# Attention over 384 short heads: loads as fp32 on the sync queue in chunks of 32 heads, casts on GpSimd, groups of 8 heads with wide evacuations and a three-stage pipeline

## The chip, the cores and the metric

The kernel runs on one core of a Trainium2 chip. The metric is device time in microseconds, the median of several runs.

The engines are PE (TensorE, matmuls and transposes; PEld is its weight load), DVE (VectorE), ACT (ScalarE), POOL (GpSimd) and SP (SyncE, which only issues DMAs here). Data move between HBM and SBUF through 16 DMA engines. "Sync queue", "scalar queue" and "GpSimd queue" say which engine issued a DMA; a DMA that changes the data type is issued from GpSimd in these kernels.

## The reference

```python
batch, n_heads, seq, head_dim = 32, 12, 128, 64     # fp32 inputs, drawn times 0.1
scores = scale * np.matmul(q, k.transpose(0, 1, 3, 2))
attn = np.exp(scores - scores_max)
attn = attn / (np.sum(attn, axis=-1, keepdims=True) + 1e-8)
return np.matmul(attn, v).astype(np.float32)
```

There are 384 heads of 128 x 64. A row of a head is 64 fp32, so 256 bytes; with the sequence on the 128 partitions, each partition reads one 256-byte run per head. Three inputs and one output make 50.33 MB.

## The kernel before

One batch entry (12 heads) at a time: casting DMAs bring q, k and v to SBUF as bf16. Pairs of heads are transposed by PE, the transposes copied out of PSUM one by one (q by ACT, k by DVE), scores formed transposed for four heads, one exp over them, outputs for two heads at a time with a 65th column of ones in v that yields the sum of the row, and one division at the end.

```python
    q_bf = pbf.tile([128, H, D], bf16, tag="q_bf")
    nc.gpsimd.dma_start(out=q_bf, in_=qr[b])             # casts while it moves; k and v alike
    for p in range(NP):
        nc.tensor.transpose(qt_ps, q_bf[:, p * HT:(p + 1) * HT, :]..., ident)
        nc.scalar.copy(qt[:, p, :], qt_ps)               # 128 x 128
        nc.tensor.transpose(kt_ps, k_bf[...], ident)
        nc.vector.tensor_copy(kt[:, p, :], kt_ps)
    for g in range(H // HX):                             # HX = 4
        ...                                              # four matmuls into sT_ps
        nc.scalar.activation(out=attnT, in_=sT_ps[:, :, :128], func=Exp, scale=scale)
        for gg in range(HX // HO):                       # HO = 2
            ...                                          # two matmuls into o_ps
            nc.vector.tensor_copy(o_b[...], o_ps[:, :, :D + 1])
    nc.vector.reciprocal(recip, o_b[:, :, D:D + 1])
    nc.vector.tensor_mul(o_sb, o_b[:, :, :D], recip.to_broadcast([128, H, D]))
    nc.sync.dma_start(out=orr[b], in_=o_sb)
```

Every PSUM pool has one buffer. The order of instructions on each engine is chosen by the framework's scheduler.

The softmax here doesn't subtract the row's maximum and nothing guards it: scores larger than these inputs give would overflow.

## Time and profile before

| | before |
|---|---|
| device time (226.3 in the later rounds with the changed kernel) | 226.2 us |
| PE / DVE / ACT / POOL busy | 168.3 / 120.2 / 99.7 / 101.5 us |
| read from and written to HBM | 37.75 + 12.58 MB, 224 GB/s over the span |
| chain of work that ended last | PE 64%, ACT 17%, DVE 9%, DMA 2% |

Busy time adds up instructions that may wait inside the pipeline, so the chain, not the busy share, says what bounds. The lines themselves are shown in the prediction below. One more view, the page's list of DMA queues (packets, MB written, and the time that the packets took as a share of 16 engines' span):

```profile
q0 software_dynamic: 148992, 18.88, 131.9%
q1 hardware_dynamic: 49664, 12.58, 31.0%
```

q0 carries the casting loads: 147,456 data packets of 128 bytes written (256 read). q1 carries the stores, 49,152 packets of 256 bytes. The share goes above 100%, so the times of packets in one engine overlap.

### The profile page before, as it was taken

The page shows a single profiled execution, that of the slowest core. Times are in us where ns is not written, and L with a number is a line of the kernel's source. Part 1 is how long each engine was busy: PE and PEld are TensorE (multiplying, and loading weights), DVE is VectorE, ACT ScalarE, POOL GpSimd, SP SyncE. Part 2 cuts the span into 40 slices and gives each one's busy share as a digit, 9 for nine tenths or more (in the row PEclk, how much of TensorE's full clock was granted, in tenths as well). Part 3 has the DMA queues.
Part 4 walks back from the last instruction along what each step waited for, and adds up shares of the span by engine and source line. Part 5 has one row for each costly group of instructions (what it writes and reads, how often), then busy time and mean ns, then how long its engine had stood idle before and what let it go on. Part 6 is the DMA issues. An engine that isn't in the chain of part 4 may idle for free.

```text
span 224.4 us, 3513 instructions
## 1 busy us (share of the span) xinstructions
PE 168.3 (75%) x1152; PEld 83.1 (37%) x1152; DVE 120.2 (54%) x448; ACT 99.7 (44%) x289; POOL 101.5 (45%) x134
## 2 busy tenths in 40 slices
PE   0688787788787787877787877788877778878750
PEld 0344333344333343333343333444333334333330
DVE  0264555664555564555564555565555565456652
ACT  2554545445544445444445444444444444444320
POOL 8963455534475443455443455543355534222000
DMA  7999999999999999999999999999999999999333
GB/s 50 149 156 184 148 142 140 155 148 166 151 153 161 161 159 166 148 149 141 129 151 167 146 148 134 137 154 167 149 146 144 135 150 161 142 110 134 76 69 71
DMA packets 198674, 31.69 MB, mean 141 GB/s; under 512 B 198656, under 2 KB 198656, under 8 KB 198656
## 3 DMA queue, kind: packets, MB, share of 16 engines
q0 software_dynamic: 148992, 18.88, 131.9%
q1 hardware_dynamic: 49664, 12.58, 31.0%
q8 instruction: 9, 0.15, 0.3%
q14 instruction: 9, 0.07, 0.1%
HBM read 37.75 MB, written 12.58 MB: 224 GB/s over the span
## 4 chain that ended last, share of the span: by engine, by line
PE 64%; ACT 17%; DVE 9%; issue 6%; DMA 2%; ACTq 0%; POOL 0%; POOLq 0%
PE sT_ps L84 26%; PE qt_ps L63 14%; PE o_ps L103 14%; PE kt_ps L70 11%; ACT attnT L92 9%; ACT qt L68 7%; DVE o_b L110 5%; DVE kt L75 3%; DMA q_bf<-in_q_dram 2%; DVE o_sb L118 1%; ACTq L92 0%; DVE recip L116 0%; POOL ident masks.py:197 0%; POOLq masks.py:199 0%; POOLq L134 0%
## 5 line engine op out<-in xcount | busy, mean ns | idle before, releaser
L68 ACT COPY qt<-qt_ps 128x128 bf16<-128x128 bf16 x192 | 50.4, 263 | 69.0 <-PE qt_ps L63 69.0
L75 DVE COPY kt<-kt_ps 128x128 bf16<-128x128 bf16 x192 | 42.8, 223 | 70.8 <-PE kt_ps L70 66.1
L84 PE MATMUL sT_ps<-qt,kt 64*128 64x128 bf16 x384 | 71.5, 282 | 12.2 <-ACT attnT L92 11.5
L92 ACT ACTIVATE attnT<-sT_ps 128x512 bf16<-128x512 f32 x96 | 57.3, 597 | 47.7 <-PE sT_ps L84 42.9
L63 PE MATMUL qt_ps<-ident,q_bf 128*128 128x128 bf16 x192 | 54.2, 282 | 26.8 <-ACT qt L68 21.4
L110 DVE COPY o_b<-o_ps 128x130 f32<-128x130 f32 x192 | 55.6, 289 | 29.2 <-PE o_ps L103 28.9
L103 PE MATMUL o_ps<-v_bf,attnT 128*128 128x65 bf16 x384 | 56.8, 242 | 6.1 <-DVE o_b L110 6.1
L70 PE MATMUL kt_ps<-ident,k_bf 128*128 128x128 bf16 x192 | 56.4, 294 | 5.3 <-DVE kt L75 4.5
L84 PEld LDWEIGHTS <-kt 64*128 64x128 bf16 x384 | 26.4, 101 | 61.1 <-issue 43.0
L103 PEld LDWEIGHTS <-attnT 128*128 128x128 bf16 x384 | 34.3, 120 | 34.4 <-issue 26.5
L56 POOL MEMSET v_bf<- 128x12 bf16 x32 | 5.0, 155 | 79.9 <-PE o_ps L103 79.9
L52 POOL DMA_DIRECT2D q_bf<-in_q_dram x32 | 32.6, 1020 | 10.2 <-PE qt_ps L63 8.9
L57 POOL DMA_DIRECT2D v_bf<-in_v_dram x32 | 32.6, 1018 | 9.9 <-POOL v_bf L56 9.9
L54 POOL DMA_DIRECT2D k_bf<-in_k_dram x32 | 32.8, 1025 | 1.4 <-PE kt_ps L70 1.4
L63 PEld LDWEIGHTS <-q_bf 128*128 128x128 bf16 x192 | 18.9, 113 | 31.4 <-issue 15.7
L118 DVE TENSOR_TENSOR o_sb<-o_b,recip 128x768 f32<-128x768 f32 x32 | 30.3, 948 | 0.0
L70 PEld LDWEIGHTS <-k_bf 128*128 128x128 bf16 x192 | 23.2, 121 | 8.7 <-issue 0.9
L116 DVE RECIPROCAL recip<-o_b 128x12 f32<-128x12 f32 x32 | 7.0, 219 | 0.0
L68 ACT ACT_TABLE_LOAD x1 | 1.3, 1283 | 0.7 <-PEq L134 0.7
masks.py:199 POOL TENSOR_SCALAR_AFFINE_SELECT ident<-ident 128x128 bf16<-128x128 bf16 x1 | 0.3, 305 | 0.1
masks.py:197 POOL MEMSET ident<- 128x128 bf16 x1 | 0.2, 204 | 0.3 <-POOLq L134 0.3
L134 POOL MEMSET const-float32-0.0<- 128x1 f32 x1 | 0.1, 98 | 0.2 <-issue 0.2
(3 smaller groups left out, 0.3 us busy)
## 6 DMA issues: line engine op xcount, KB each, us to landing
out_dram<-o_sb SPq DMA_DIRECT2D x32, 384.0 KB, 5.7
q_bf<-in_q_dram POOLq DMA_DIRECT2D x32, 192.0 KB, 5.9
k_bf<-in_k_dram POOLq DMA_DIRECT2D x32, 192.0 KB, 6.4
v_bf<-in_v_dram POOLq DMA_DIRECT2D x32, 192.0 KB, 5.1
```

What stands on the lines that cost most here:

```text
L52: nc.gpsimd.dma_start(out=q_bf, in_=qr[b])
L54: nc.gpsimd.dma_start(out=k_bf, in_=kr[b])
L57: nc.gpsimd.dma_start(out=v_bf[:, :, :D], in_=vr[b])
L63: nc.tensor.transpose(qt_ps, q_bf[:, p * HT:(p + 1) * HT, :].rearrange("a b c -> a (b c)"), ident,)
L68: nc.scalar.copy(qt[:, p, :], qt_ps)
L70: nc.tensor.transpose(kt_ps, k_bf[:, p * HT:(p + 1) * HT, :].rearrange("a b c -> a (b c)"), ident,)
L75: nc.vector.tensor_copy(kt[:, p, :], kt_ps)
L84: nc.tensor.matmul(sT_ps[:, i, :128], lhsT=kt[j * D:(j + 1) * D, p, :], rhs=qt[j * D:(j + 1) * D, p, :], start=True, stop=True,)
L92: nc.scalar.activation(out=attnT, in_=sT_ps[:, :, :128], func=mybir.ActivationFunctionType.Exp, bias=0.0, scale=scale,)
L103: nc.tensor.matmul(o_ps[:, i, :D + 1], lhsT=attnT[:, gg * HO + i, :], rhs=v_bf[:, h, :], start=True, stop=True,)
L110: nc.vector.tensor_copy(o_b[:, g * HX + gg * HO:g * HX + (gg + 1) * HO, :], o_ps[:, :, :D + 1],)
L118: nc.vector.tensor_mul(o_sb, o_b[:, :, :D], recip.to_broadcast([128, H, D]))
```

## The change

Its intent is to replace many small instructions by few wide ones and to keep loads off GpSimd's queue. Loads become fp32 DMAs of 32 heads on the sync queue, with a cast by GpSimd after each. Groups of 8 heads are evacuated at once: one copy of 1024 bf16 for the transposes, one exp over 1024, one reciprocal and one multiplication straight from PSUM. Transposes of group s, scores of group s-1 and outputs of group s-2 follow each other in a fixed order. Stores also go by the sync queue, and the loads of chunk c+3 stand behind the store of chunk c.

```diff
-        nc.gpsimd.dma_start(out=q_bf, in_=qr[b])
+            nc.sync.dma_start(out=x, in_=src[:, sl, :])          # x: fp32, 32 heads
...
+        nc.gpsimd.tensor_copy(q_bf, q_f)                         # k and v alike
...
-            nc.scalar.copy(qt[:, p, :], qt_ps)
-            nc.vector.tensor_copy(kt[:, p, :], kt_ps)
+            nc.vector.tensor_copy(qkt, t_ps)                     # 8 heads of q and k
...
-                nc.vector.tensor_copy(o_b[...], o_ps[:, :, :D + 1])
+            nc.vector.reciprocal(recip, ov[:, :, :, D])
+            nc.vector.tensor_mul(o_sb[...], ov[:, :, :, :D], recip.to_broadcast([128, 2, HP, D]))
+            if r == GPC - 1:
+                nc.sync.dma_start(out=orr[:, c * CH:(c + 1) * CH, :], in_=o_sb)
+                if c + 3 < NCH:
+                    load(c + 3)
+        for s in range(NG + 2):
+            if s < NG:
+                stage_a(s)                                       # transposes, one copy
+            if 0 <= s - 1 < NG:
+                stage_b(s - 1)                                   # scores, exp
+            if 0 <= s - 2 < NG:
+                stage_c(s - 2)                                   # outputs, division
```

(The transposes and scores have two PSUM buffers, the outputs one.)

More of the change, by code (lines that the diff above doesn't have):

```diff
@@ L26, with heads @@
     scale = 1.0 / (D ** 0.5)
-    HT = 128 // D
-    NP = H // HT
-    HX = 4
-    HO = 2
-    BANK = 512
-    qr = q.rearrange("b h s d -> b s h d")
-    kr = k.rearrange("b h s d -> b s h d")
-    vr = v.rearrange("b h s d -> b s h d")
-    orr = out.rearrange("b h s d -> b s h d")
-    singles = ctx.enter_context(tc.tile_pool(name="singles", bufs=1))
+    N = B * H
+    CH = 32
+    NCH = N // CH
+    GH = 8
+    NG = N // GH
+    GPC = CH // GH
+    HP = GH // 2
+    def heads(x):
+        return x.rearrange("b h s d -> s (b h) d")
@@ new lines @@
+    qr, kr, vr, orr = heads(q), heads(k), heads(v), heads(out)
+    singles = ctx.enter_context(tc.tile_pool(name="singles", bufs=1))
+    pin = ctx.enter_context(tc.tile_pool(name="pin", bufs=3))
+    pbf = ctx.enter_context(tc.tile_pool(name="pbf", bufs=3))
+    pt = ctx.enter_context(tc.tile_pool(name="pt", bufs=3))
+    pa = ctx.enter_context(tc.tile_pool(name="pa", bufs=3))
+    po = ctx.enter_context(tc.tile_pool(name="po", bufs=3))
+    ps_t = ctx.enter_context(tc.tile_pool(name="ps_t", bufs=2, space=bass.MemoryType.PSUM))
@@ L39 @@
+    ps_s = ctx.enter_context(tc.tile_pool(name="ps_s", bufs=2, space=bass.MemoryType.PSUM))
+    ps_o = ctx.enter_context(tc.tile_pool(name="ps_o", bufs=1, space=bass.MemoryType.PSUM))
     ident = singles.tile([128, 128], bf16)
     make_identity(nc, ident)
-    pbf = ctx.enter_context(tc.tile_pool(name="pbf", bufs=3))
-    pt = ctx.enter_context(tc.tile_pool(name="pt", bufs=3))
-    pa = ctx.enter_context(tc.tile_pool(name="pa", bufs=6))
-    po = ctx.enter_context(tc.tile_pool(name="po", bufs=2))
@@ L46 @@
-    ps_t = ctx.enter_context(tc.tile_pool(name="ps_t", bufs=1, space=bass.MemoryType.PSUM))
-    ps_s = ctx.enter_context(tc.tile_pool(name="ps_s", bufs=1, space=bass.MemoryType.PSUM))
-    ps_o = ctx.enter_context(tc.tile_pool(name="ps_o", bufs=1, space=bass.MemoryType.PSUM))
-    for b in range(B):
-        q_bf = pbf.tile([128, H, D], bf16, tag="q_bf")
-        nc.gpsimd.dma_start(out=q_bf, in_=qr[b])
-        k_bf = pbf.tile([128, H, D], bf16, tag="k_bf")
-        nc.gpsimd.dma_start(out=k_bf, in_=kr[b])
-        v_bf = pbf.tile([128, H, D + 1], bf16, tag="v_bf")
-        nc.gpsimd.memset(v_bf[:, :, D:D + 1], 1.0)
-        nc.gpsimd.dma_start(out=v_bf[:, :, :D], in_=vr[b])
-        qt = pt.tile([128, NP, 128], bf16, tag="qt")
-        kt = pt.tile([128, NP, 128], bf16, tag="kt")
-        for p in range(NP):
-            qt_ps = ps_t.tile([128, 128], bf16, tag="qt_ps")
-            nc.tensor.transpose(
-                qt_ps,
-                q_bf[:, p * HT:(p + 1) * HT, :].rearrange("a b c -> a (b c)"),
-                ident,
-            )
-            nc.scalar.copy(qt[:, p, :], qt_ps)
-            kt_ps = ps_t.tile([128, 128], bf16, tag="kt_ps")
-            nc.tensor.transpose(
-                kt_ps,
-                k_bf[:, p * HT:(p + 1) * HT, :].rearrange("a b c -> a (b c)"),
-                ident,
-            )
-            nc.vector.tensor_copy(kt[:, p, :], kt_ps)
-        o_b = po.tile([128, H, D + 1], f32, tag="o_b")
-        for g in range(H // HX):
-            sT_ps = ps_s.tile([128, HX, BANK], f32, tag="sT")
-            for i in range(HX):
-                h = g * HX + i
-                p, j = divmod(h, HT)
-                nc.tensor.matmul(
-                    sT_ps[:, i, :128],
-                    lhsT=kt[j * D:(j + 1) * D, p, :],
-                    rhs=qt[j * D:(j + 1) * D, p, :],
-                    start=True,
-                    stop=True,
-                )
-            attnT = pa.tile([128, HX, 128], bf16, tag="attnT")
-            nc.scalar.activation(
-                out=attnT,
-                in_=sT_ps[:, :, :128],
-                func=mybir.ActivationFunctionType.Exp,
-                bias=0.0,
-                scale=scale,
-            )
-            for gg in range(HX // HO):
-                o_ps = ps_o.tile([128, HO, BANK], f32, tag="o_ps")
-                for i in range(HO):
-                    h = g * HX + gg * HO + i
-                    nc.tensor.matmul(
-                        o_ps[:, i, :D + 1],
-                        lhsT=attnT[:, gg * HO + i, :],
-                        rhs=v_bf[:, h, :],
-                        start=True,
-                        stop=True,
-                    )
-                nc.vector.tensor_copy(
-                    o_b[:, g * HX + gg * HO:g * HX + (gg + 1) * HO, :],
-                    o_ps[:, :, :D + 1],
-                )
-        recip = po.tile([128, H], f32, tag="recip")
-        nc.vector.reciprocal(recip, o_b[:, :, D:D + 1])
-        o_sb = po.tile([128, H, D], f32, tag="o_sb")
-        nc.vector.tensor_mul(o_sb, o_b[:, :, :D], recip.to_broadcast([128, H, D]))
-        nc.sync.dma_start(out=orr[b], in_=o_sb)
@@ new lines, with load, cast @@
+    chunks = {}
+    raw = {}
+    def load(c):
+        sl = slice(c * CH, (c + 1) * CH)
+        tiles = []
+        for src, tag in ((qr, "q_f"), (kr, "k_f"), (vr, "v_f")):
+            x = pin.tile([128, CH, D], f32, tag=tag, name=tag)
+            nc.sync.dma_start(out=x, in_=src[:, sl, :])
+            tiles.append(x)
+        raw[c] = tiles
+    def cast(c):
+        q_f, k_f, v_f = raw.pop(c)
+        q_bf = pbf.tile([128, CH, D], bf16, tag="q_bf", name="q_bf")
+        nc.gpsimd.tensor_copy(q_bf, q_f)
+        k_bf = pbf.tile([128, CH, D], bf16, tag="k_bf", name="k_bf")
+        nc.gpsimd.tensor_copy(k_bf, k_f)
+        v_bf = pbf.tile([128, CH, D + 1], bf16, tag="v_bf", name="v_bf")
+        nc.gpsimd.memset(v_bf[:, :, D:D + 1], 1.0)
+        nc.gpsimd.tensor_copy(v_bf[:, :, :D], v_f)
+        chunks[c] = (q_bf, k_bf, v_bf)
@@ new lines, with stage_a, stage_b, stage_c @@
+    with tc.manual_schedule():
+        qkts, attns, osbs = {}, {}, {}
+        for c in range(3):
+            load(c)
+        cast(0)
+        def stage_a(i):
+            c, r = divmod(i, GPC)
+            q_bf, k_bf, v_bf = chunks[c]
+            t_ps = ps_t.tile([128, 2, HP, 128], bf16, tag="t_ps", name="t_ps")
+            for p in range(HP):
+                for j, x in enumerate((q_bf, k_bf)):
+                    h = GH * r + 2 * p
+                    nc.tensor.transpose(
+                        t_ps[:, j, p, :], x[:, h:h + 2, :].rearrange("p h d -> p (h d)"), ident)
+            qkt = pt.tile([128, 2, HP, 128], bf16, tag="qkt", name="qkt")
+            nc.vector.tensor_copy(qkt, t_ps)
+            qkts[i] = qkt
+        def stage_b(i):
+            qkt = qkts.pop(i)
+            s_ps = ps_s.tile([128, 2, HP, 128], f32, tag="s_ps", name="s_ps")
+            for p in range(HP):
+                for j in range(2):
+                    pr = slice(j * D, (j + 1) * D)
+                    nc.tensor.matmul(s_ps[:, j, p, :], lhsT=qkt[pr, 1, p, :],
+                                     rhs=qkt[pr, 0, p, :], start=True, stop=True)
+            attn = pa.tile([128, 2, HP, 128], bf16, tag="attn", name="attn")
+            nc.scalar.activation(out=attn, in_=s_ps, func=mybir.ActivationFunctionType.Exp,
+                                 bias=0.0, scale=scale)
+            attns[i] = attn
+        def stage_c(i):
+            c, r = divmod(i, GPC)
+            attn = attns.pop(i)
+            v_bf = chunks[c][2]
+            o_ps = ps_o.tile([128, 2, 512], f32, tag="o_ps", name="o_ps")
+            ov = o_ps[:, :, :HP * (D + 1)].rearrange("p j (h e) -> p j h e", h=HP)
+            for h in range(GH):
+                nc.tensor.matmul(ov[:, h // HP, h % HP, :], lhsT=attn[:, h % 2, h // 2, :],
+                                 rhs=v_bf[:, GH * r + h, :], start=True, stop=True)
+            if r == 0:
+                osbs[c] = po.tile([128, CH, D], f32, tag="o_sb", name="o_sb")
+            o_sb = osbs[c]
+            recip = pa.tile([128, 2, HP], f32, tag="recip", name="recip")
+            nc.vector.reciprocal(recip, ov[:, :, :, D])
+            nc.vector.tensor_mul(
+                o_sb[:, GH * r:GH * (r + 1), :].rearrange("p (j h) d -> p j h d", j=2),
+                ov[:, :, :, :D], recip.to_broadcast([128, 2, HP, D]))
+            if r == GPC - 1:
+                nc.sync.dma_start(out=orr[:, c * CH:(c + 1) * CH, :], in_=o_sb)
+                osbs.pop(c)
+                if c + 3 < NCH:
+                    load(c + 3)
+        for s in range(NG + 2):
+            if s % GPC == 0 and s // GPC + 1 < NCH:
+                cast(s // GPC + 1)
+            if s < NG:
[4 more added lines that the diff above has]
+                stage_c(s - 2)
```

## The prediction

> **What bounds the kernel now.** I read the page's busy shares and the chain of work that ended last, then the list of waits, then the groups, and last the stretches of time with their DMA rates.
>
> ```profile
> PE 168.3 (75%) x1152; PEld 83.1 (37%) x1152; DVE 120.2 (54%) x448; ACT 99.7 (44%) x289; POOL 101.5 (45%) x134
> ...
> PE 64%; ACT 17%; DVE 9%; issue 6%; DMA 2%; ACTq 0%; POOL 0%; POOLq 0%
> PE sT_ps L84 26%; PE qt_ps L63 14%; PE o_ps L103 14%; PE kt_ps L70 11%; ACT attnT L92 9%; ACT qt L68 7%; DVE o_b L110 5%; DVE kt L75 3%; DMA q_bf<-in_q_dram 2%; DVE o_sb L118 1%; ACTq L92 0%; DVE recip L116 0%; POOL ident masks.py:197 0%; POOLq masks.py:199 0%; POOLq L134 0%
> ```
>
> No engine is full, and DMA is 2% of the chain. The chain alternates between PE and an evacuation: PE writes a PSUM tile, ACT or DVE copies it out, and PE waits for that copy, because each of the four PSUM tiles has one buffer. The kernel is bound by a latency chain of small instructions. The waits agree: PE waits for ACT qt 21.4 us, for ACT attnT 11.5, for DVE o_b 6.1, for DVE kt 4.5. In the loads it is the other way round, POOL waits for PE to free a buffer:
>
> ```profile
> POOL v_bf L56 <- PE o_ps L103: 79.9, 29, 4.2
> ```
>
> So loads are not late today. But the DMA engines are not far from full: 50.33 MB cross HBM in 224.4 us, all in pieces of 256 B. Four stretches of time (columns: start and end in us, length, busy us of PE, PEld, DVE, ACT and POOL with counts, granted clock, DMA share, GB/s) show what they can do:
>
> ```profile
> 14.00:16.00 2.00, 1.82 (x15) 0.82 (x13) 1.19 (x6) 1.08 (x4) 1.08 (x3) 1.00 2.44 156
> 20.80:21.60 0.80, 0.63 (x8) 0.38 (x6) 0.44 (x2) 0.75 (x2) 0.00 (x0) 1.00 1.36 272
> 221.30:222.90 1.60, 0.00 (x0) 0.00 (x0) 0.00 (x0) 0.00 (x0) 0.00 (x0) 1.00 1.11 218
> ...
> 206.00:206.50 0.50, 0.50 (x4) 0.23 (x3) 0.28 (x2) 0.00 (x0) 0.00 (x0) 1.00 1.35 272
> ```
>
> The first is a backlog of casting loads, before the first store moves; its rate stays at 156 GB/s from 10 to 20 us, so it is a ceiling. The rate counts the 128 B written, so it is 16 x 128 B / 156 GB/s = 13.1 ns per packet and DMA engine. The third is the last store alone, on the sync queue: 16 x 256 B / 218 GB/s = 18.8 ns per packet. The second and the fourth are mostly stores while the last loads run out: 16 x 256 B / 272 = 15.1 ns if all were stores. So a 256-byte packet costs an engine 13 to 19 ns, and the kernel after has exactly as many of them.
>
> **What the Trainium skill says.** "DMA: Bandwidth & Descriptors", section "Why small descriptors are slow (HBM only)": a 256-byte descriptor takes 256/32 + 3 = 11 cycles. The section "Specifications" of the same page gives 850 MHz, so 12.9 ns; the 13.1 ns of the casting loads agree. It also says that below 512 B the engine reads, modifies and writes; 18.8 ns is 16 such cycles, which would fit that for the stores, while 15.1 ns speaks against it as a rule. No trace here shows a 256-byte load from the sync queue. "GPSIMD Engine Reference", section "Performance pitfalls for Q7 kernels": about 1.9 cycles per element where the reading steps are small (the engine runs at 1.2 GHz). Here the 128x128 mask instruction took 305 ns and a 128x128 memset 204, so 1 to 2 cycles per element fit; a cast of 2048 elements is not in this trace. "SBUF — State Buffer", section "Who interferes with whom": only DVE instructions in a 2-port mode or with two SBUF inputs block GpSimd. The changed kernel's DVE work all reads PSUM, so I count no blocking; L118, which did have two SBUF inputs, is gone.
>
> **The change part by part.**
>
> *Evacuations.* Read from the groups:
>
> ```profile
> L68 ACT COPY qt<-qt_ps 128x128 bf16<-128x128 bf16 x192 | 50.4, 263 | 69.0 <-PE qt_ps L63 69.0
> L75 DVE COPY kt<-kt_ps 128x128 bf16<-128x128 bf16 x192 | 42.8, 223 | 70.8 <-PE kt_ps L70 66.1
> L92 ACT ACTIVATE attnT<-sT_ps 128x512 bf16<-128x512 f32 x96 | 57.3, 597 | 47.7 <-PE sT_ps L84 42.9
> L110 DVE COPY o_b<-o_ps 128x130 f32<-128x130 f32 x192 | 55.6, 289 | 29.2 <-PE o_ps L103 28.9
> L118 DVE TENSOR_TENSOR o_sb<-o_b,recip 128x768 f32<-128x768 f32 x32 | 30.3, 948 | 0.0
> ```
>
> L75 and L110 differ by 66 ns with nearly the same element count: with a common fixed part near 155 ns, bf16 from PSUM goes at 0.52 ns and fp32 at 1.04 ns per element. Per group of 8 heads DVE then needs: one copy of 1024 bf16, 155 + 533 = 0.69 us; one reciprocal of 8, about 0.24 (L116 takes 0.22 for 12); one multiplication of 512 fp32 from PSUM, 155 + 533 = 0.69. Sum 1.62 us, 48 groups: 78 us instead of 120. ACT: exp of 1024; 597 ns less 512/1.2 GHz leaves 170 ns fixed, so 1.02 us, 48 times 49 us instead of 100. The copies of L68 and L110 go.
>
> *PE.* The same 1152 matmuls. In the chain of before, in order of time, two scores matmuls advance it by 0.22 us, so 0.11 each where nothing holds it; 24 per group are 2.64 us, 127 us in all. The order of instructions shows transposes of group s, scores of s-1, outputs of s-2 in turn, with two buffers for transposes and scores; each evacuation has a step of 2.64 us to hide in, and none needs more than 1.62. The chain that bounds the kernel now is broken. Compute alone would take 48 x 2.64 = 127 us and a few for filling.
>
> *Casts.* 36 of 2048 elements. At 1.9 cycles, 2048 x 1.9 / 1.2 GHz = 3.24 plus 0.1, so 3.3 us (an estimate from the GPSIMD page); three per chunk of 32 heads are 10 us, 120 us in all, beside the rest. The 96 DMA issues of 1.02 us leave POOL (98 us).
>
> *DMA.* 147,456 load and 49,152 store packets as before, 9,216 and 3,072 per engine. Now all are on the sync queue, whose order is fixed: nine loads, then store of chunk c and the three loads of chunk c+3. A load behind a store waits until that chunk is computed, but two more chunks are queued by then. A chunk's packets (768 + 256) take 13.4 us at 13.1 ns and 19.3 us at 18.8, against 4 x 2.64 = 10.6 us on PE and 10 on POOL. So DMA becomes the bound. Store of chunk c needs the k cast of chunk c+1 and six stages after it (about 5 us); that is 8 us after k of chunk c+1 landed, while the queue still holds v, a store and the whole next chunk (1280 packets, at least 16.8 us). So it never runs dry.
>
> *Sum.* Start until bytes flow: 1.8 us (SP is free at 0.7 us, and the last store of before moved 1 us after its issue). Until the last v lands: 9,216 loads and the stores of chunks 0 to 8, 2,304. I take 14.5 ns for a load (between 13.1, casting, and 15.1) and 17.5 for a store (between 15.1 and 18.8): 133.6 + 40.3 = 173.9 us. Tail: the last k is cast when v lands; four steps of 2.64, two partial steps (2.6) and reciprocal with multiplication (0.9) are 14; then the last store of 256 packets: 1.0 + 4.5 + 1.3 (before, bytes ended at 223.1 of 224.4) = 6.8. Total 1.8 + 173.9 + 14 + 6.8 = 196.5, rounded to 196.
>
> **The rivals.**
> (a) *Sync-queue loads cost what the lone store cost, 18.8 ns.* For it: loads now write 256 B instead of 128, and the only lone sync-queue transfer ran so. Against it: the 272 GB/s, which the same queue reached with little else running. It would make 1.8 + 216.6 + 21 = 239 us, slower.
> (b) *Loads cost 13.1 ns as the casting ones do and stores 15.1.* 1.8 + 120.7 + 34.8 + 21 = 178 us.
> (c) *Casts are slow.* At 4.5 us each, POOL needs 13.5 us per chunk, about as much as DMA at its fastest: 162 us in all plus start and tail, some 190. It bounds only above 5.5 us; at 7 us it would be 252 plus 25. The 1.9 cycles speak against that, and no run here has a cast.
> (d) *DMA is no bound and the pipeline is*: if one PSUM buffer for outputs makes every step wait for the multiplication (0.9 us more), 48 x 3.6 = 173 us plus 25, hence near 198; it would hide behind DMA anyway.
>
> **Range and chances.** Nearly all uncertainty is nanoseconds per load packet: one ns is 9.2 us. From 13.1 to 15.6 for loads, with stores between 15.1 and 18.8, spans 178 to 210; 17 ns for both gives 219. The limit for over 2% faster, 221.7 us, is met below about 17.3 ns for all packets. I give that 0.80, rival (a) or worse 0.12, the rest between. Eight in ten: 172 to 228.
>
> **What would show it.** Right: the chain of the changed kernel ends mostly in DMA and what waits for it; PE's longest waits go to the casts, the casts' to the loads; DMA moves an even 230 to 310 GB/s from 2 us to about 175; DVE near 78 us, ACT near 49; casts near 3.3 us. Wrong: a DMA rate that falls to zero between chunks (the queue runs dry), a rate of 218 GB/s throughout (rival a), POOL over 90% busy (c), or PE waiting for DVE and ACT rather than for casts (d).

## The result, and the profile after

The changed kernel takes 232.0 us against 226.3 in the same rounds: 2.6% slower (ratio 1.026, 95% interval 1.0244 to 1.0277). Ratios here are the mean time of one kernel's fast runs over that of the other's of the same rounds, so not quite the ratio of the medians. The time lies outside the predicted range, and in the other direction.

These are lines of the page of the changed kernel: busy time, the granted clock in 40 slices, packets, the DMA queue, the chain that ended last, and the groups.

```profile
PE 84.4 (37%) x1152; PEld 64.4 (28%) x1152; DVE 73.4 (32%) x144; ACT 50.4 (22%) x49; POOL 71.0 (31%) x54
...
PEclk9999999566569557558759656656955755875665
...
DMA packets 86797, 50.51 MB, mean 219 GB/s; under 512 B 49920, under 2 KB 86784, under 8 KB 86784
...
q1 hardware_dynamic: 86784, 50.33, 104.2%
...
SPq 43%; DMA 40%; POOL 4%; issue 4%; PE 3%; DVE 2%; POOLq 0%
...
L106 ACT ACTIVATE attn<-s_ps 128x1024 bf16<-128x1024 f32 x48 | 49.1, 1023 | 169.4 <-PE s_ps L103 168.8
L94 DVE COPY qkt<-t_ps 128x1024 bf16<-128x1024 bf16 x48 | 33.0, 688 | 135.0 <-PE t_ps L91 135.0
L91 PE MATMUL t_ps<-ident,q_bf 128*128 128x128 bf16 x192 | 40.0, 280 | 73.7 <-POOL q_bf L70 73.7
...
L70 POOL CAST q_bf<-q_f 128x2048 bf16<-128x2048 f32 x12 | 22.7, 1893 | 80.8 <-DMA q_f<-in_q_dram 80.8
...
L124 DVE TENSOR_TENSOR o_sb<-o_ps,recip 128x512 f32<-128x512 f32 x48 | 33.2, 691 | 1.7
```

The busy time of PE and ACT fell to half, that of DVE to 61%. The chain of before ran through PE; this one runs through the sync queue and DMA for 83%. The waits read backwards tell the same story: PE waits for the casts, the casts wait for the loads. All 50.33 MB are on q1. The loads are counted here as 36,864 packets of 1 KB. Why is not shown; the access pattern in the program still reads runs of 256 bytes.

The DMA rate by stretches, before (one stretch) and after (three; columns as in the prediction):

```profile
60.00:100.00 40.00, 31.74 (x218) 15.63 (x217) 22.44 (x85) 18.59 (x55) 20.09 (x25) 1.00 1.81 156
```

```profile
20.00:30.00 10.00, 3.20 (x38) 2.46 (x35) 2.41 (x5) 1.02 (x1) 3.97 (x3) 1.00 1.11 218
60.00:100.00 40.00, 14.02 (x192) 10.69 (x192) 12.20 (x24) 8.18 (x8) 12.98 (x9) 0.63 1.08 228
...
120.00:128.00 8.00, 4.90 (x86) 3.75 (x80) 5.84 (x12) 4.09 (x4) 1.89 (x1) 0.88 1.12 251
```

Before, the rate counts 128 bytes per load packet, so 156 GB/s is more traffic than it looks. After, every byte counts at full width: with loads alone exactly the 218 GB/s that the lone store showed before, and a little more (251) in the stretch around a switch between loads and stores. The queue never runs dry. It is busy from the first to the last slice, at a rate that is too low: 50.33 MB at 228 GB/s are 221 us.

### The profile page after: what moved, and what is told of

Its sections match the earlier page's. It is cut to its first block, busy times and chain, and to the rows that moved or that the text cites. A ratio compares the mean times of both kernels' runs of the same rounds, so it can differ in the third digit from the quotient of the medians.

```text
span 230.2 us, 2848 instructions
## 1 busy us (share of the span) xinstructions
PE 84.4 (37%) x1152; PEld 64.4 (28%) x1152; DVE 73.4 (32%) x144; ACT 50.4 (22%) x49; POOL 71.0 (31%) x54
## 3 DMA queue, kind: packets, MB, share of 16 engines
q1 hardware_dynamic: 86784, 50.33, 104.2%
## 4 chain that ended last, share of the span: by engine, by line
SPq 43%; DMA 40%; POOL 4%; issue 4%; PE 3%; DVE 2%; POOLq 0%
DMA k_f<-in_k_dram 40%; SPq L63 38%; SPq L128 4%; POOL k_bf L72 4%; DVE o_sb L124 1%; PE o_ps L117 1%; PE t_ps L91 1%; PE s_ps L103 1%; DVE recip L123 0%; POOL v_bf L74 0%; DVE qkt L94 0%; POOLq L72 0%
## 5 line engine op out<-in xcount | busy, mean ns | idle before, releaser
L106 ACT ACTIVATE attn<-s_ps 128x1024 bf16<-128x1024 f32 x48 | 49.1, 1023 | 169.4 <-PE s_ps L103 168.8
L94 DVE COPY qkt<-t_ps 128x1024 bf16<-128x1024 bf16 x48 | 33.0, 688 | 135.0 <-PE t_ps L91 135.0
L91 PE MATMUL t_ps<-ident,q_bf 128*128 128x128 bf16 x192 | 40.0, 280 | 73.7 <-POOL q_bf L70 73.7
L91 PE MATMUL t_ps<-ident,k_bf 128*128 128x128 bf16 x192 | 39.1, 281 | 56.1 <-POOL k_bf L72 56.1
L70 POOL CAST q_bf<-q_f 128x2048 bf16<-128x2048 f32 x12 | 22.7, 1893 | 80.8 <-DMA q_f<-in_q_dram 80.8
L72 POOL CAST k_bf<-k_f 128x2048 bf16<-128x2048 f32 x12 | 22.7, 1893 | 36.7 <-DMA k_f<-in_k_dram 36.7
L124 DVE TENSOR_TENSOR o_sb<-o_ps,recip 128x512 f32<-128x512 f32 x48 | 33.2, 691 | 1.7
L75 POOL CAST v_bf<-v_f 128x2048 bf16<-128x2048 f32 x12 | 22.7, 1892 | 26.3 <-DMA v_f<-in_v_dram 26.3
L117 PE MATMUL o_ps<-v_bf,attn 128*128 128x65 bf16 x384 | 25.2, 220 | 8.0 <-DVE o_sb L124 6.9
L103 PE MATMUL s_ps<-qkt 64*128 64x128 bf16 x384 | 25.2, 270 | 0.1
L123 DVE RECIPROCAL recip<-o_ps 128x8 f32<-128x8 f32 x48 | 10.0, 208 | 13.1 <-PE o_ps L117 12.9
```

The costliest lines, as they stand in the source:

```text
L70: nc.gpsimd.tensor_copy(q_bf, q_f)
L72: nc.gpsimd.tensor_copy(k_bf, k_f)
L75: nc.gpsimd.tensor_copy(v_bf[:, :, :D], v_f)
L91: nc.tensor.transpose(t_ps[:, j, p, :], x[:, h:h + 2, :].rearrange("p h d -> p (h d)"), ident)
L94: nc.vector.tensor_copy(qkt, t_ps)
L103: nc.tensor.matmul(s_ps[:, j, p, :], lhsT=qkt[pr, 1, p, :], rhs=qkt[pr, 0, p, :], start=True, stop=True)
```

## The experiments

The two kernels of DMA alone, and the one without most loads, give wrong outputs on purpose. The two of DMA alone ran once each, so their state is unknown; their rates for 256-byte runs agree with those inside the whole kernels (218 GB/s as fp32, 156 to 157 as casts). Each ratio is to the kernel before on the same chip in the same call; where two runs of different calls are compared, that kernel's medians of 226.3 to 226.8 us tell how far this can be trusted.

### The evacuation half, with the loads out of the way

```diff
-                if c + 3 < NCH:
-                    load(c + 3)
+                if c + 3 < NCH:
+                    raw[c + 3] = kept[c % 3]       # cast the tiles of chunks 0 to 2 again
```

> The changed kernel that loads only its first three chunks and casts those again for the others; stores as changed; wrong result on purpose. It shows what the evacuation half is worth with the loads out of the way. If the pipeline runs as predicted (up to 2.64 us of PE per group, DVE 1.62), 48 groups take 127 us at most, plus about 25 for start and tail: 110 to 155 us. If the one PSUM buffer of the outputs serialises (rival d, 3.6 us per group), about 195 us.

Measured: 121.5 us (ratio 0.536 from the fast runs; one of the four was slow). One stretch of it, well inside its steady part:

```profile
45.00:90.00 45.00, 35.57 (x686) 27.92 (x684) 42.08 (x85) 28.73 (x29) 43.16 (x31) 0.96 0.82 177
```

DVE is busy 42.08 of 45 us (POOL too, casting ahead), and the granted clock is back near 1. So the pipeline as such is worth a great deal, it would be bound by DVE at the 1.6 us per group that the prediction worked out, and the single PSUM buffer of the outputs (rival d) is not the bound: PE waits for it 14.4 us in all. The 121.5 us are not compute alone: until 45 us the nine loads of the first three chunks still arrive, at 218 GB/s. By 48 groups of 1.6 us, compute alone would be some 77 us and a few for filling (an estimate). The loss comes from the loads.

### The two halves, each alone

First the changed kernel with casting loads put back:

```diff
-            nc.sync.dma_start(out=x, in_=src[:, sl, :])
+        nc.gpsimd.dma_start(out=q_bf, in_=qr[:, sl, :])   # k and v alike; no cast on GpSimd
```

> The changed kernel with its loads undone: 32-head casting loads on the GpSimd queue, no casts on GpSimd, all the rest as changed. If the sync queue's 18.8 ns per run is the cause, loads fall to 13.1 ns per run (120.7 us) and stores run partly beside them: 14 to 15 ns per run over all, 172 to 184 us of DMA plus about 20 us of start and tail, so 185 to 205 us. If HBM or the pipeline is the limit, it stays within 2% of 232.

Measured: 208.6 us (ratio 0.921, 0.9192 to 0.9228), correct. Undoing the load half alone turns 2.6% slower into 7.9% faster. It is 3.6 us above the range that was expected, 185 to 205. From the page of that kernel, the DMA share in 40 slices and the queues:

```profile
DMA  4999999999999999999999999999999999994566
...
q0 software_dynamic: 148032, 18.88, 142.1%
q1 hardware_dynamic: 49344, 12.58, 38.7%
```

DMA is still the bound: its engines are busy from the second slice until the last loads, and PE waits 56.7 us for the k loads and 30.2 for the q loads. (The chain that ended last puts 59% on "issue", so it does not show this.) The run of DMA alone below shows why it is not faster: a store between casting loads costs more than a store by itself.

Then the kernel before with the load half only:

```diff
-        nc.gpsimd.dma_start(out=q_bf, in_=qr[b])
+        q_f = pin.tile([128, H, D], f32, tag="q_f")        # pin: 3 buffers
+        nc.sync.dma_start(out=q_f, in_=qr[b])
+        nc.gpsimd.tensor_copy(q_bf, q_f)                   # k and v alike
```

> The kernel before with only the load half of the change: 12-head fp32 loads on the sync queue and casts on GpSimd, its small evacuations kept. With 18.8 ns per run for loads and stores the data alone need 231 us, so 240 to 260 us: slower than before by 6 to 15%. If the load half were harmless, 226 us would stay.

Measured: 353.6 us (ratio 1.56). This was far off, and it is not DMA time: its queue moves 143 GB/s in the mean and its chain holds little DMA.

```profile
PE 41%; ACT 19%; DVE 17%; issue 10%; DMA 6%; POOL 5%; SPq 1%; POOLq 0%; ACTq 0%
```

The order of its PE instructions differs. This is the sequence of matmuls on PE over one batch entry, counted by output tile, in the two programs:

```
before:      sT 2, kt 1, sT 2, qt 1, o 2, kt 1, sT 1, o 2, sT 1, qt 3, sT 2, kt 1, o 2, ...
loads only:  sT 4, o 10, qt 1, o 2, qt 5, kt 2, sT 2, kt 1, sT 2, kt 1, sT 1, kt 1, sT 3, ...
```

Ten output matmuls in a row share one PSUM buffer, so each pair waits for its copy with little between. The scheduler chose that order. A rival stands beside it, in the waits of the sync queue:

```profile
SPq L126 <- DVE o_sb L125: 195.3, 31, 10.0
```

The stores stand in the queue of the loads, which wait behind them for the division. Of PE's idle time 134 us end with an evacuation by ACT or DVE and 23 with a cast, so the order seems to weigh more. The next run moves the stores to another queue and adds load buffers, which brings an alternating order back:

```diff
-        nc.sync.dma_start(out=orr[b], in_=o_sb)
+        nc.scalar.dma_start(out=orr[b], in_=o_sb)          # and pin with 6 buffers
```

> The load half of the change alone again (it took 353.6 us, where its ten output matmuls in a row wait for the one PSUM buffer, an order that the scheduler chose), now with the stores on the scalar queue and six load buffers, which gives back an instruction order that alternates like that of the kernel before. If the order made the 353 us, it falls below 260 us; the data alone need 173 us for loads at 18.8 ns. If the loads themselves did, it stays above 300.

Measured: 249.9 us (ratio 1.102). As this edit changed three things at once (queue, buffers, order), the share of each in the 104 us between the two runs is not separated; that the order made most of it is argued, not shown. The 249.9 us are again a chain of PE, DVE and ACT. What can be said is that the load half alone is no gain in either form.

### What a run of consecutive bytes costs

The next kernel only moves data, in stretches with a barrier between them.

```python
for i in range(3): nc.sync.dma_start(out=X[i], in_=heads(...)[:, 32 heads, :])         # 256-byte runs
for i in range(3): nc.sync.dma_start(out=..., in_=pairs(...))                          # 512-byte runs
for i in range(3): nc.sync.dma_start(out=..., in_=flat(...))                           # 8-KB runs
for i in range(3): nc.sync.dma_start(...); nc.scalar.dma_start(...)                    # 256, two queues
for i in range(3): nc.gpsimd.dma_start(out=X[i], ...)                                  # 256, no cast
for i in range(3): nc.gpsimd.dma_start(out=Y[i], ...)                                  # 256, cast to bf16
...                                                                                    # stores, mixtures
```

> DMA alone, in eleven stretches with a barrier between them; the outputs are wrong on purpose. Theory G (a hardware queue hands out one 256-byte run per 18.8 ns and engine, however long the data): sync loads in 256-byte runs at 218 GB/s, 512-byte runs and 8-KB runs well above it (300 GB/s or more). Rival B (the queue is limited in bytes, 13.6 GB/s per engine): 218 GB/s for all three. Rival H (HBM does not read 256-byte runs faster than this with full-width writes): the GpSimd queue without a cast also moves 218; under G it moves about 310 (13.1 ns per run). For two hardware queues at once (sync and scalar): 218 GB/s if they share what hands out the runs, 280 or more if each has its own. Stores in 256-byte runs 218, in 512-byte runs above 300 under G.

Six stretches from the inside of the first six, in that order, then casting loads and stores together:

```profile
22.00:32.00 10.00, 0.31 (x2) 0.00 (x0) 0.00 (x0) 1.00 1.11 218
39.00:46.00 7.00, 0.31 (x2) 0.00 (x0) 0.00 (x0) 1.00 1.06 290
52.00:58.00 6.00, 0.31 (x2) 0.00 (x0) 0.00 (x0) 1.00 1.00 422
66.00:86.00 20.00, 0.31 (x2) 0.34 (x1) 0.00 (x0) 1.00 1.11 217
98.00:107.00 9.00, 0.31 (x2) 0.00 (x0) 0.00 (x0) 1.00 1.03 218
116.00:124.00 8.00, 0.31 (x2) 0.00 (x0) 0.72 (x1) 1.00 2.46 157
...
172.00:182.00 10.00, 0.15 (x1) 0.00 (x0) 0.00 (x0) 1.00 1.76 158
```

(Columns: start and end, length, busy time of DVE, ACT and POOL, clock, DMA share, GB/s written.)

- 256-byte runs as fp32: 218 GB/s from the sync queue, 217 from two hardware queues together, and 218 from the GpSimd queue. Theory G, that the hardware queue hands out runs too slowly, falls with the last of these: it had expected 310 there. The cost belongs to the copy, not to the queue.
- The same runs cast to bf16: 157 GB/s written, so 314 read. HBM can read 256-byte runs that fast, so reading is not the limit. Rival H had added "with full-width writes", and its test came out as it said (218 from the GpSimd queue), so it falls only for the reading; that the bytes written are not what costs is shown by the second kernel below.
- Longer fp32 runs are faster: 290 GB/s at 512 bytes, 422 at 8 KB. Rival B, a limit in bytes, falls. Stores alone: 216 at 256 bytes (128 to 134 us) and 283 at 512 (137.2 to 140.8 us), where G had expected above 300.
- Casting loads and stores taking turns: 158 GB/s with 384 bytes per pair, so 16 x 384 / 158 = 38.9 ns for the two. Less 13.0 for the load, a store beside casting loads costs 25.9 ns instead of 18.8 (which of the two pays more was not separated). That is why casting loads did not gain more in the kernel: 9,216 x 13.0 + 3,072 x 25.9 = 199 us of DMA work, for a run of 208.6.

A second kernel of this kind varied the length of a run:

> DMA alone again, nine stretches; wrong outputs on purpose. The first such run gave, per run of consecutive bytes and engine, 18.8 ns for 256 B fp32 on either queue, 13.1 for 256 B cast to bf16, about 28 for 512 B fp32[...]. Theory W (a run costs about 7.3 ns plus the bytes written at 22.4 B per ns and engine): cast 512 B read 18.7 ns, cast 1 KB 30 ns, sync 1 KB 53 ns, sync 128 B 13.0 ns, stores of 1 KB 53 ns. Rival R (the longer of what is read and what is written counts, and a cast is cheap only because it is packed otherwise): cast 512 B 28 ns, sync 128 B still near 13 or more. Casting loads of 512 B beside stores: sums of the single costs if the engine is one resource.

Stretches of casting loads with 512 bytes, 1 KB and 8 KB read per run, sync loads in runs of 128 bytes, stores in runs of 1 KB, sync loads beside scalar stores in runs of 512 bytes, and casting loads of 512 bytes beside stores of 256 (columns without ACT):

```profile
23.00:28.00 5.00, 0.31 (x2) 0.00 (x0) 1.00 1.81 180
36.00:40.00 4.00, 0.15 (x1) 0.00 (x0) 1.00 1.45 196
48.00:52.00 4.00, 0.31 (x2) 0.00 (x0) 1.00 1.06 213
...
69.00:74.00 5.00, 0.16 (x2) 0.00 (x0) 1.00 1.23 194
...
80.00:82.00 2.00, 0.01 (x1) 0.00 (x0) 1.00 1.05 347
...
111.00:120.00 9.00, 0.31 (x2) 0.00 (x0) 1.00 1.08 374
...
134.00:144.00 10.00, 0.31 (x2) 0.00 (x0) 1.00 1.47 170
```

Turned into time per run and engine (16 x bytes written / rate), and into cycles of 1.18 ns, which is the 850 MHz that the Trainium skill's page "DMA: Bandwidth & Descriptors" gives in its section "Specifications":

| bytes read per run | fp32 copy | cycles | bytes/32 + 8 | cast to bf16 | cycles | bytes/32 + 3 |
|---|---|---|---|---|---|---|
| 128 | 10.6 ns | 9.0 | 12 | not run | | 7 |
| 256 | 18.8 ns | 16.0 | 16 | 13.0 ns | 11.1 | 11 |
| 512 | 28.2 ns | 24.0 | 24 | 22.8 ns | 19.3 | 19 |
| 1,024 | 47.2 ns (store) | 40.1 | 40 | 41.8 ns | 35.5 | 35 |

Theory W, bytes written plus 7.3 ns, expected 18.7 and 30 ns for the casts of 512 bytes and 1 KB; 22.8 and 41.8 refute it. Rival R expected 28 ns for the cast of 512 bytes, and falls too. What is read counts. The casting loads follow the skill's own formula for a 256-byte descriptor (same page, section "Why small descriptors are slow (HBM only)": bytes/32 plus about 3 cycles) at all three lengths. Plain fp32 copies fit bytes/32 + 8 at 256, 512 and 1,024 bytes, but not at 128: 10.6 ns, 9.0 cycles where the fit has 12 (both theories had expected 13 ns or more). So a 256-byte run pays 5 cycles, 5.8 ns, more as fp32 than as a cast. The fit is a description of three lengths; which part of the DMA engine spends the 5 cycles was not found.

The last stretch repeats what mixing costs: if casting loads of 512 bytes and stores of 256 take turns, a pair takes 16 x 512 / 170 = 48.2 ns, where the single costs add up to 41.6. The expectation of plain sums fails here as it did with 38.9 against 31.8 before.

### Two queues

The changed kernel with the k loads on the scalar engine's queue:

```diff
+            eng = nc.scalar if tag == "k_f" else nc.sync
-            nc.sync.dma_start(out=x, in_=src[:, sl, :])
+            eng.dma_start(out=x, in_=src[:, sl, :])
```

> The changed kernel with the k loads on the scalar engine's hardware queue. If each hardware queue has its own limit of 18.8 ns per run, two together reach 13 to 15 ns and the time falls to 185 to 205 us. If both share one limit, 232 us stays within 2%, or rises by a few us, since a load issue holds the scalar engine for about 4 us.

Measured: 231.5 us (ratio 1.022), as good as no change. Two queues that both load share one limit, as the 217 GB/s above say. In this run the stores on the sync queue also stand beside k loads on the scalar queue for part of the time, and single slices reach 295 GB/s; yet the mean of the page is 221 GB/s against 219.

The same with the stores, not the loads, on the scalar queue:

```diff
-                nc.sync.dma_start(out=orr[:, c * CH:(c + 1) * CH, :], in_=o_sb)
+                nc.scalar.dma_start(out=orr[:, c * CH:(c + 1) * CH, :], in_=o_sb)
```

> The changed kernel with the stores on the scalar engine's queue instead of behind the loads on the sync queue. Theory: the 16 DMA engines are the bound and each packet costs the same on any queue: within 2% of 232 us. Rival: reading and writing HBM at once overlap (some stretches of the DMA-only run moved 270 to 300 GB/s with loads and stores together), then 185 to 210 us.

Measured: 217.1 us (ratio 0.960, 0.9582 to 0.9618), correct. One word in the program turns 2.6% slower into 4.0% faster. The theory (each packet costs the same on any queue) falls; the rival was right in kind, though its range ended at 210. The stretch of 512-byte loads beside 512-byte stores shows it most clearly: 374 GB/s against 290 for loads alone, so 16 x 512 / 374 = 21.9 ns per run, 18.6 cycles instead of 24. The first DMA-only kernel had the same at 256 bytes: sync loads beside scalar stores, and then, from 157.5 to 160.5 us, a store of the scalar queue (landed at 160.6) beside one of the sync queue (issued at 157.4). Both move some 290 GB/s, against 218 for loads and 216 for stores from one queue:

```profile
150.00:156.00 6.00, 0.08 (x1) 0.00 (x0) 0.00 (x0) 1.00 1.17 290
...
157.50:160.50 3.00, 0.00 (x0) 0.00 (x0) 0.00 (x0) 1.00 1.27 289
```

In stretches of the kernel with its stores on the scalar queue:

```profile
60.00:70.00 10.00, 6.88 (x83) 5.54 (x85) 4.56 (x10) 3.07 (x3) 3.96 (x3) 0.50 1.15 269
100.00:110.00 10.00, 2.18 (x41) 1.54 (x37) 3.47 (x7) 2.16 (x3) 3.72 (x2) 0.81 1.17 270
```

The reading is that stores in the queue of the loads are moved one after the other, and that from a second queue they go between the loads; the traces show the rates, not the order of packets. The skill's page "DMA: Bandwidth & Descriptors", section "Issuing engines are not separate DMA queues", says that initiating DMAs on several engines only saves the sequencer's time. For two loading queues the runs agree (217 GB/s, 231.5 us), for a loading and a storing queue they do not (374 GB/s, 217.1 us).

### Longer runs in the real kernel

If the cost sits in each run, halving the number of runs must pay. Two neighbouring rows of a head are 512 consecutive bytes. So q, k and out are moved with two rows per partition and two heads over the 128 partitions. The transposes are done in 64 x 64 pieces, and the k columns are put back into their order by the copy out of PSUM. The output matmuls are split in two by rows (not in the cut below). v stays as it was, so three of four tensors have 512-byte runs.

```diff
+    def pairs(x):
+        return x.rearrange("b h s d -> (b h s d)").rearrange("(n p e) -> p n e", p=128, e=2 * D)
...
+                    for e in range(2):
+                        for t in range(2):
+                            pr = slice(t * D, (t + 1) * D)
+                            nc.tensor.transpose(t_ps[pr, j, p, e * D:(e + 1) * D],
+                                x[pr, HP * r + p, e * D:(e + 1) * D], ident[pr, pr])
...
+            nc.vector.tensor_copy(qkt[:, 0], t_ps[:, 0])
+            nc.vector.tensor_copy(qkt[:, 1].rearrange("x h (s e) -> x h s e", e=2),
+                                  t_ps[:, 1].rearrange("x h (e s) -> x h s e", e=2))
```

Once with the stores on the sync queue:

> As e6_pairs, but the stores stay behind the loads on the sync queue. If one queue is served one run after the other, the stores add 1,536 runs of 28.2 ns per engine, 43 us: 200 to 215 us, and the difference from the changed kernel (232) is what longer runs are worth alone. If the queue of the stores makes no difference, as e6_pairs.

Measured: 200.6 us (ratio 0.885, 0.8834 to 0.8861), correct. And once with the stores on the scalar queue:

> The changed kernel with q, k and out moved in runs of 512 B (two rows of a head in a partition, two heads over 128 partitions, the transposes in 64x64 pieces, the k columns put back in order by the evacuation) and the stores on the scalar queue; v stays at 256 B. DMA theory (a sync-queue run costs bytes/32 + 8 cycles of 1.18 ns, so 18.8 ns at 256 B and 28.2 at 512; stores from a second queue go nearly for free beside loads): per chunk 2 x 128 x 28.2 + 256 x 18.8 = 12.0 us, 144 us for all loads, plus 2 and about 20 for start and tail: 165 to 185 us. Rival: bytes bound, 217 us as with stores on the scalar queue alone. PE and DVE have 2.2 and 2.0 us per group to do, 106 and 97 us in all, below either.

Measured: 181.6 us (ratio 0.801, 0.7993 to 0.8023), correct, inside the range expected, though 16 us above its sum of 144 + 2 + 20: stores beside loads are cheaper here, not free. This beats both kernels, with 2,688 PE instructions instead of 1,152. Two lines of its page and one stretch:

```profile
PE 88.4 (49%) x2688; PEld 73.3 (41%) x2688; DVE 88.7 (49%) x192; ACT 50.4 (28%) x49; POOL 71.1 (40%) x54
...
SPq 80%; issue 6%; DMA 5%; DVE 3%; POOLq 1%; PE 1%; POOL 0%
```

```profile
80.00:120.00 40.00, 21.37 (x672) 17.59 (x666) 22.18 (x48) 12.29 (x12) 17.44 (x12) 0.76 1.08 310
```

Its queue moves 310 GB/s where the changed kernel's moved 228, and it is still bound by the loads. The steps add up, nearly: longer runs alone take 31.4 us off (232.0 to 200.6), a queue of their own for the stores 14.9 (to 217.1), both 50.4 (to 181.6).

| kernel | us | ratio to before |
|---|---|---|
| before | 226.3 | 1 |
| the change | 232.0 | 1.026 |
| k loads on the scalar queue | 231.5 | 1.022 |
| stores on the scalar queue | 217.1 | 0.960 |
| casting loads, rest as changed | 208.6 | 0.921 |
| 512-byte runs for q, k, out | 200.6 | 0.885 |
| the same, stores on the scalar queue | 181.6 | 0.801 |
| load half alone, in two forms | 353.6; 249.9 | 1.562; 1.102 |
| loads of three chunks only | 121.5 | 0.536 |

## Why the prediction was wrong

**What bounds the kernel before** was read correctly: with the chain of small evacuations broken and most loads gone, the kernel takes 121.5 us. But it stood closer to its next bound than its chain shows: the same loads without that chain still take 208.6 us.

**Evacuations.** Predicted 78 us for DVE and 49 for ACT, measured 73.4 and 50.4. The single instructions fit: 0.69 us for the wide copy and for the multiplication, 1.02 for the exp (0.60 before, for half the elements).

**PE.** Predicted 2.64 us per group; in the last chunk a group took about 1.95 us, with PE busy throughout at a granted clock of 0.50 (213.5 to 217.4 us), and 1.6 us, bound by DVE, in the run without most loads at 0.96. So the lower clock may have cost the last chunk some 0.35 us per group (an estimate). Before it PE waits for casts, not for DVE or ACT.

**Casts.** Predicted 3.3 us, measured 1.89. The step was too high by three quarters, with little effect on the sum, since the casts lie beside the loads. The prediction counted no blocking of GpSimd by DVE, and all 36 casts took 1.89 us. Where DVE does multiply two SBUF tiles, in the load-half runs (L125), a cast of 768 elements that begins during it took 1.56 us instead of 0.83 (at 163.2 us of the 353.6 us run), as the page that the prediction names for it states.

**DMA becomes the bound, and its queue does not run dry.** Both right: 83% of the chain is the sync queue and DMA, and no slice is below 140 GB/s.

**The sum.** This is the step that failed, and in one term: "I take 14.5 ns for a load (between 13.1, casting, and 15.1) and 17.5 for a store". The last v landed at 213.5 us, when its cast began, and the last store was issued at 223.2 (views of the two tiles, changed kernel):

```profile
L75 POOL CAST v_bf<-v_f x12: 1892/1892/1892, 17.8 to 213.5; 128x2048 bf16<-128x2048 f32 x12
```

```profile
L128 SPq DMA_DIRECT2D out_dram<-o_sb x12: 372/4672/4868, 39.9 to 223.2; - x12
```

From 1.8 to 213.5 us the queue served 9,216 loads and 2,304 stores per engine: 211.7 / 11,520 = 18.4 ns each, where the prediction had 173.9 us, 15.1 ns. That is 37.8 us. It is the loads that were mis-sized: with nothing else in the queue (20 to 30 us, 218 GB/s) a load took 18.8 ns, not 14.5, which is 39.6 us for 9,216. The tail was 4.1 us shorter than predicted (230.2 - 213.5 = 16.7 against 20.8), and 1.8 us between the span and the device time had been left out. 37.8 - 4.1 + 1.8 = 35.5 of the 36.0 us that are missing; the rest is rounding.

Rival (a) was the right one, given 0.12: fp32 loads cost what the lone store cost. Two readings misled. The casting loads' 13.1 ns was taken to be what a 256-byte read costs, but a cast has 5 cycles less per run than a copy. The page's 11 cycles, and the estimate of 12.9 ns from them, agreed with the casts and said nothing of the copies to come. And 272 GB/s "with little else running" was taken to speak for the sync queue; in the DMA-only run the same queue held 218 GB/s over long stretches of loads. In those 0.5 and 0.8 us the last casting loads of another queue ran beside the stores; whether that made the 272 was not tested. The evidence that decided was in the profile of before, the lone store at 218 GB/s: the one transfer that had the width and the queue of the new loads.

**So where did the expected gain go?** The evacuation half takes compute out of the way (121.5 us with most loads gone). The load half raises the DMA work from 9,216 x 13.0 + 3,072 x 25.9 = 199 us (loads and stores on two queues, mixed) to 12,288 x 18.8 = 231 us (one queue), and that became the bound.

## What to carry to other kernels

When a change moves the bound to DMA, count runs of consecutive bytes, not megabytes, and take the cost of a run from a transfer of the same width, type and queue; a casting load is no measure for a plain one. For plain fp32 loads, try longer runs and a queue of their own for the stores: here these two steps took 50 us off the changed kernel, while the rewrite of the compute, with the loads left as they were, took 17.7 off the one before. Beside casting loads a store was dearer, not cheaper, so this is no rule for them. And test a rewrite half by half, since one half can hide what the other is worth.

## What the Trainium skill lacked or had wrong

- "DMA: Bandwidth & Descriptors", section "Why small descriptors are slow (HBM only)": bytes/32 plus about 3 cycles holds for casting loads (13.0, 22.8 and 41.8 ns for 256, 512 and 1,024 bytes), but plain fp32 copies, loads and stores, fit about 8 (18.8, 28.2, 47.2 ns; at 128 bytes 10.6 ns, about 5). No page tells the two apart.
- The same page, section "Specifications", sets a limit of 512 bytes below which an engine reads, modifies and writes. No step is seen there for fp32 copies: the extra is the same 8 cycles at 256, 512 and 1,024 bytes, and smaller at 128.
- The same page, section "Issuing engines are not separate DMA queues": true for two loading queues (217 GB/s), not for loads and stores on two queues (374 GB/s against 290 at 512 bytes, 290 against 218 at 256; 217.1 us against 232.0 in the kernel).
- "GPSIMD Engine Reference", section "Performance pitfalls for Q7 kernels": the 1.9 cycles per element stand there for kernels with short reading steps, and were no measure for a cast of fp32 to bf16. Casts of 768 and 2,048 elements that nothing held up took 0.83 and 1.89 us, so 0.83 ns per element, one cycle at the page's 1.2 GHz.
- No page: a store between casting loads of the GpSimd queue costs 25.9 ns per 256 bytes, by itself 18.8.
- No page: 256-byte stores run at 216 GB/s from one queue and at 289 while two queues store (157.5 to 160.5 us of the first DMA-only run); two queues that load stay at 217. Nor is it explained why loads and stores of one queue are faster for some two us where they take turns (251 GB/s in the stretch of the changed kernel shown above).
